# Means of squares: two rounded products with the split squares in place of one float32 product, in a two-layer hybrid trunk

## The chip, the cores and the metric

The kernel runs on 1 core of one Trainium2 chip. The metric is the device time of one execution in microseconds (us). Every row below is from the hardware profile of one execution; PE is TensorE, PEld its weight loads, DVE is VectorE, ACT is ScalarE, POOL is GpSimd, SP is SyncE, which here issues DMAs only.

## The reference, cut to what matters

Two layers over one sequence of 512 tokens of width 1024, all in float32:

```python
for l in range(2):
    x = x + 0.5 * swiglu(rms_norm(x, ffn1_norm[l]), ffn1_w_in[l], ffn1_w_out[l])   # hidden width 2816
    h = rms_norm(x, mix_norm[l]) @ w_mix_in[l]
    y = concat[short_conv(h parts), hgrn2(h parts), forgetting_attention(h parts)]
    x = x + y @ w_mix_out[l]
    x = x + 0.5 * swiglu(rms_norm(x, ffn2_norm[l]), ffn2_w_in[l], ffn2_w_out[l])

def rms_norm(x, gain):
    return x * rsqrt(mean(x * x, axis=-1) + 1e-6) * gain
# hgrn2 ends, for each of 4 heads of width 64:  rms_norm(o, out_gain) * silu(gate)
```

So there are six norms of x (two feed-forwards and a mixer in each of two layers), and a norm of HGRN2's heads in each layer.

## The kernel before

x is held transposed: 8 tiles `xT` of 128 features by 512 tokens, so a mean over features is a sum over partitions, which TensorE does as a product with a matrix of constants (`ones_mean`, 1/1024 everywhere; `ones_blk`, 1/64 in two diagonal blocks, one for each head of a pair).

Large products don't run in float32. Each operand is taken apart into a high part, the value rounded to the type F32R (fp32r in the profile), and a low part, what is missing: a cast on ACT, then a subtraction on DVE (`parted`, lines 398 and 401, for a weight tile `st` into `hl`). A product is then three rounded ones, high x high, low x high, high x low (`mm3`, lines 413, 419, 420). Weights come in pairs of 128 rows: one DMA into the staging buffer `st` (two of these), one cast, one subtraction into `hl` (three of these), and 24 products of 512 columns.

The squares of x are not taken apart. `norm_part` makes, for tile j, the operand's high part `x` = gain * xT on ACT (line 537), its low part on DVE (538), the square on ACT (548 for the first tile, 551 for the others) and on DVE the running sum `sqa` (552). `sum_norm` (line 571) then is one float32 product `ones_mean` x `sqa`, and `take_norm` makes the inverse root of it on ACT and DVE. The scale `inv` is applied to the products behind it, so the products with weights start before the norm is known:

- In a mixer, `features` streams the first four weight pairs, and the sum (`end_norm`) stands ahead of the last pair's products.
- In a feed-forward, `cover` works through the first hidden tiles with pairs of weight rows. Ahead of pair n, `deal(n)` places work by hand: the sum (`squares`) where n is `mean`, which is 2 in the first feed-forward and 3 in the second one; the norm, the other operands and so on from a table by pair.
- In the very first feed-forward of the kernel (`begin` given) the norm has a path of its own.

What sets the order: each engine works through its own queue in program order. `follow` chains instructions of one engine in the order in which the code makes them; in `cover`, the weights' casts and subtractions (`keep` in `parted`), the products and what `deal` places are chained so, while `norm_part`'s squares are placed by the scheduler. Elsewhere the weights' rounding has a high priority, and the scheduler takes it as early as its buffers allow.

The HGRN2 part (`hgrn`) runs as a generator for each pair of heads, beside the attention's projections. It ends with `sq`, the squares of the output, a float32 product `ones_blk` x `sq` (line 1479), the inverse root (`r`, `t`; line 559 is its first DVE step), and the output's two parts `hy`. Behind it in program order comes the attention: the operands `b` from transposes (1597, 1598), DMA copies of them by SP's queue (1605), scores (1632), their negative row maximum `nm` on DVE (1646), the exponential `P` on ACT (309), the values `V` (1570, scaled by `invc` on DVE), transposes (1669) and the products with V (1687).

PSUM holds eight banks under four names, `mm` (3), `sc` (2), `pt` (2) and `po` (1); a product into a bank waits until its former reader is done.

Of the kernel before, what the change touches and what calls it, by code (L numbers as in the profile page):

```python
# [8 lines left out]
F32 = mybir.dt.float32  # L9
F32R = mybir.dt.float32r  # L10
# [15 lines left out]
P = 128  # L26
T = 512
D = 1024
# [155 lines left out]
class Trunk:  # L184
# [8 lines left out]
    def __init__(self, ctx, tc):  # L193
        self.tc = tc
        self.nc = tc.nc
        nc = self.nc
        self.uid = 0
        self.ntog = 0
        self.tab, self.tab_users = None, []
        self.chain = {}  # L200
        self.hl0 = None
        self.const = ctx.enter_context(tc.tile_pool(name="const", bufs=1))
        self.res = ctx.enter_context(tc.tile_pool(name="res", bufs=1))
        self.wp = ctx.enter_context(tc.tile_pool(name="wp", bufs=1))
        self.ps = ctx.enter_context(
            tc.tile_pool(name="ps", bufs=1, space=bass.MemoryType.PSUM)
        )
        self.dram = ctx.enter_context(
            tc.tile_pool(name="dram", bufs=1, space=bass.MemoryType.DRAM)
        )  # L210

        self.none = self.res.tile([P, T], F32R, tag="inv", name="none")
        self.follow("v", nc.vector.memset(self.none.bitcast(F32), 0.0))
        self.ident = self.const.tile([P, P], F32, tag="ident", name="ident")
        make_identity(nc, self.ident)
        self.ones_mean = self.const.tile([P, P], F32, tag="ones_mean", name="ones_mean")
        self.follow("v", nc.vector.memset(self.ones_mean, 1.0 / D))
        self.epsc = self.const.tile([P, 1], F32, tag="epsc", name="epsc")
        nc.vector.memset(self.epsc, EPS)
        self.xT = self.res.tile([P, KD, T], F32, tag="xT", name="xT")  # L220

        self.xh, self.xl = [None] * KD, [None] * KD

    def build_consts(self, scratch):

        nc = self.nc
        c = self.const

        self.ones_blk = c.tile([P, P], F32, tag="ones_blk", name="ones_blk")
        nc.vector.memset(self.ones_blk, 0.0)  # L230
        for h in range(2):
            nc.vector.memset(self.ones_blk[64 * h : 64 * h + 64, 64 * h : 64 * h + 64], 1.0 / 64)

        self.heads2 = c.tile([P, 2], F32, tag="heads2", name="heads2")
        nc.vector.memset(self.heads2, 0.0)
        for h in range(2):
            nc.vector.memset(self.heads2[64 * h : 64 * h + 64, h : h + 1], 1.0)

        self.smask = c.tile([P, T], F32, tag="smask", name="smask")
        nc.vector.memset(self.smask, 1.0)  # L240
        nc.vector.memset(self.smask.rearrange("p (c t) -> p c t", t=CH)[:, :, 0:1], 0.0)
        self.identb = c.tile([P, P], BF16, tag="identb", name="identb")
        nc.vector.tensor_copy(self.identb, self.ident)
        self.utri = c.tile([P, T], F32R, tag="utri", name="utri")
        self.maskb = c.tile([P, P], BF16, tag="maskb", name="maskb")

        self.lmask = c.tile([P, 6, CH], U8, tag="lmask", name="lmask")
        self.same = c.tile([P, CH], F32, tag="same", name="same")
        ft = scratch(I32)[:, :P]
        pt = scratch(I32)[:, :P]  # L250
        nc.gpsimd.iota(ft, pattern=[[1, P]], base=0, channel_multiplier=0)
        nc.gpsimd.iota(pt, pattern=[[0, P]], base=0, channel_multiplier=1)
        ftf = scratch(F32)[:, :P]
        ptf = scratch(F32)[:, :P]
        nc.vector.tensor_copy(ftf, ft)
        nc.vector.tensor_copy(ptf, pt)
        x = scratch(I32)[:, :P]
        nc.vector.tensor_tensor(x, ft, pt, op=ALU.bitwise_xor)
        xf = scratch(F32)[:, :CH]
        later = scratch(F32)[:, : P + CH]  # L260
        later, own = later[:, :P], later[:, P:]
        nc.vector.tensor_tensor(later, ftf, ptf, op=ALU.is_gt)
        for h in range(2):

            r = slice(CH * h, CH * h + CH)
            nc.vector.tensor_copy(xf[r], x[r, r])
            nc.vector.tensor_copy(own[r], later[r, r])
            nc.vector.tensor_copy(self.same[r], self.ident[r, r])
        a = scratch(F32)[:, :CH]
        b = scratch(F32)[:, :CH]  # L270
        for l in range(1, 7):
            i = nc.vector.tensor_scalar(
                a, xf, scalar1=float(2 ** (l - 1)), scalar2=None, op0=ALU.is_ge
            )
            if l == 1:

                self.tc.add_manual_dep(i.ins, self.first_rows, NOSYNC, reason="opening order")
            nc.vector.tensor_scalar(b, xf, scalar1=float(2**l), scalar2=None, op0=ALU.is_lt)
            nc.vector.tensor_mul(a, a, b)
            nc.vector.tensor_mul(self.lmask[:, l - 1, :], a, own)  # L280

        nc.vector.tensor_scalar(self.maskb, later, scalar1=-1e30, scalar2=None, op0=ALU.mult)

        nc.vector.tensor_tensor(self.utri[:, :P], ftf, ptf, op=ALU.is_ge)
        of = scratch(F32)[:, P:]
        nc.vector.memset(of, 1.0)
        nc.vector.tensor_copy(self.utri[:, P:], of)
# [278 lines left out]
    def end_norm(self, bank, pool):  # L566
        self.sum_norm(bank)
        self.take_norm(bank, pool)

    def sum_norm(self, bank):  # L570
        return self.nc.tensor.matmul(bank, self.ones_mean, self.sqacc, start=True, stop=True)

    def take_norm(self, bank, pool):

# [76 lines left out]
    def cover(self, fp, w_in, w_out, covered, mean, begin):  # L651
# [3 lines left out]
        nc = self.nc  # L655
        if begin is not None:
            x, gain = begin
        A, V = (lambda i, e=e: self.follow(e, i) for e in "av")
        norm, tiles, values = [], [], {}
# [20 lines left out]
        def squares():  # L680

            norm.append(self.bank("pt" if self.ntog % 2 == 0 else "po"))
            i = self.sum_norm(norm[0])
            if begin is None:
                self.follow("p", i)

        def deal(n):
            if n == mean and begin is None:
                squares()
            for what in filter(None, ENTRY[covered].get(n, "").split(", ")):  # L690
                name, *at = what.split()
                at = [int(v) if v.isdigit() else v for v in at]
                if name == "norm":
                    for e, i in self.take_norm(norm[0], fp):
                        self.follow(e, i)
                    self.table(SILU)
                    self.signs()
                elif name == "x":
                    self.normalise(fp, *at)
                elif name == "+":  # L700
                    x, y = (self.xn[tuple(v)] for v in (at[:2], at[2:]))
                    V(nc.vector.tensor_add(x, x, y))
                elif name == "clear":
                    clear(*at)
                elif name == "silu":
                    gi = values[at[0]][0]
                    A(self.act(gi, gi, AF.Silu))
                elif name == "values":
                    value(*at)
                elif name == "load":  # L710
                    next(halved)
                elif name == "sum":
                    self.first_sum()
                else:
                    self.operand(fp, name)
# [343 lines left out]
    def mix(self, l, w, w_out, conv_w, out_gain, q_gain, k_gain, f_bias, next_gain, logits):  # L1059
        nc, tc = self.nc, self.tc  # L1060
        FM2 = [slice(0, P), slice(P, 2 * P)]
        TOK = [slice(c, c + P) for c in (0, 128, 256, 384)]
        with tc.tile_pool(name=self.n("mix"), bufs=1) as mp:
# [31 lines left out]
            def features(*args):  # L1095
                g = features_steps(*args)
                while True:
                    try:
                        next(g)
                    except StopIteration as e:  # L1100
                        return e.value
# [10 lines left out]
            with tc.tile_pool(name=self.n("hg"), bufs=1) as hp:  # L1112
                self.tt, self.tb = "t", 8

                b, kb, q, S = (pair(mp, tag) for tag in ("b", "kb", "q", "S"))
                negc = mp.tile([NH, 2, T], F32R, tag="n", name=self.n("negc"))
                bz = features([(H_F, 256)], ("mm", "mm"), lambda: self.end_norm(self.bank("pt"), hp))
                if l == 0:
                    self.lower_bounds(logits, hp.tile([P, T], F32, tag="t", name=self.n("lb"), bufs=8))
# [165 lines left out]
    def hgrn(self, l, pr, hp, z, q, q2, v, sg, og, S, kb, b):  # L1285
# [7 lines left out]
        nc = self.nc  # L1293
# [178 lines left out]
        for par in range(2):  # L1472
            mine = lambda a: a.rearrange("p (i two t) -> p i two t", two=2, t=CH)[:, :, par, :]
            src = ob[par][:, : T // 2].rearrange("p (i t) -> p i t", t=CH)
            nc.scalar.activation(mine(sq), src, AF.Square)
            nc.scalar.copy(mine(o), src)
        yield
        mb = self.bank("sc")
        nc.tensor.matmul(mb, self.ones_blk, sq, start=True, stop=True)
        self.act(r, mb, AF.Ln, bias=self.epsc)  # L1480
        self.act(r, r, AF.Exp, scale=-0.5)
        self.rsqrt(r, mb, r, t)
# [373 lines left out]
```

## Time and profile before

| | |
|---|---|
| median of 3 runs | 1824.36 us (1824.35 to 1825.08) |
| the profiled execution's own time | 1826.36 us |
| its span in the profile | 1824.6 us |
| PE busy | 1816.4 us, 13,237 products |
| PEld busy | 1662.6 us |
| DVE busy | 1436.1 us, 1,971 instructions |
| ACT busy | 1000.3 us, 1,421 instructions |
| POOL busy | 185.2 us |
| granted TensorE clock | 1.00 |
| DMA | 262.43 MB, mean 144 GB/s |

How to read it: the span is the time from the first to the last profiled event on the core. A row of a timeline has the start in us from the span's beginning, the duration, the engine, the line of the kernel, the operation, output<-inputs by the program's names, and shapes; a bracket at its end holds the engine's idle time before the row and what ended it. "x2" behind a matmul says that the instruction stands as two records. Matmuls overlap their predecessors, so what one costs is the distance to its successor's start, not its duration. An `SPq` row is a DMA issue on SP's queue.

### The profile page before, as it was taken

The numbers are of one execution on the slowest core, as the hardware profiler recorded it, in microseconds if no ns is written. First come the engines' busy times: TensorE is split into PE (matmuls) and PEld (weight loads), VectorE is DVE, ScalarE is ACT, GpSimd is POOL, SyncE is SP. The second block draws the span as 40 slices with busy tenths as digits, with TensorE's granted clock in tenths as the row PEclk, the third lists the DMA queues.
The fourth block names the chain that finished last, engine by engine and source line by source line (L and its number), as shares of the span: only waits on it lengthen the run. The fifth ranks groups of instructions, "written<-read, shape, count | busy, mean of one in ns | idle before, by whom it ended". The sixth has DMA issues, their size and how long they took to land.

```text
span 1824.6 us, 32613 instructions
## 1 busy us (share of the span) xinstructions
PE 1816.4 (100%) x13237; PEld 1662.6 (91%) x13237; DVE 1436.1 (79%) x1971; ACT 1000.3 (55%) x1421; POOL 185.2 (10%) x190
## 2 busy tenths in 40 slices
PE   9999999999999999999999999999999999999999
PEld 7899999887888899999889999998878888999998
DVE  7889787678677898879678887976777778888883
ACT  5455554465665465555445555555656655555552
POOL 0011120100000101112001111201000001020210
PEclk9999999999999999999999999999999999999999
DMA  7658784242543867868276787823425438677762
GB/s 213 179 130 193 179 177 98 66 126 78 125 105 96 223 139 163 195 162 170 81 201 140 173 182 195 162 70 77 122 79 127 120 93 219 162 153 195 155 135 93
DMA packets 249911, 262.43 MB, mean 144 GB/s; under 512 B 19816, under 2 KB 228464, under 8 KB 249760
## 3 DMA queue, kind: packets, MB, share of 16 engines
q1 hardware_dynamic: 193904, 192.15, 35.8%
q0 software_dynamic: 55840, 68.19, 23.6%
q8 instruction: 104, 1.70, 0.4%
q14 instruction: 47, 0.39, 0.1%
q10 hardware_dynamic: 16, 0.00, 0.0%
HBM read 226.15 MB, written 2.17 MB: 125 GB/s over the span
## 4 chain that ended last, share of the span: by engine, by line
PE 95%; DVE 1%; ACT 1%; DMA 1%; issue 0%; SPq 0%; ACTq 0%; DVEq 0%
PE mm L413 14%; PE mm L420 14%; PE mm L419 14%; PE sc L413 6%; PE sc L420 6%; PE sc L419 6%; PE pt L419 6%; PE pt L413 6%; PE pt L420 6%; PE po L413 4%; PE po L419 4%; PE po L420 4%; PE sc L1632 1%; PE po L1687 1%; PE pt L1669 1%; DMA st<-in_ffn_w_in_dram 1%
## 5 line engine op out<-in xcount | busy, mean ns | idle before, releaser
L865 ACT CAST hl<-w 128x1024 fp32r<-128x1024 f32 x322 | 337.7, 1050 | 349.5 <-PE mm L420 81.9
L867 DVE TENSOR_TENSOR hl<-w,hl 128x1024 fp32r<-128x1024 f32 x322 | 393.1, 1222 | 87.2 <-ACT hl L865 87.1
L401 DVE TENSOR_TENSOR hl<-st,hl 128x1024 fp32r<-128x1024 f32 (+3 forms) x152 | 160.4, 1055 | 121.7 <-ACT hl L398 121.3
L398 ACT CAST hl<-st 128x1024 fp32r<-128x1024 f32 (+3 forms) x151 | 138.2, 915 | 184.0 <-PE po L420 84.5
L413 PE MATMUL mm<-xc,hl 128*128 128x256 f32 (+1 forms) x730 | 201.3, 276 | 0.3 <-ACT g L964 0.3
L420 PE MATMUL mm<-xc,hl 128*128 128x256 f32 x728 | 201.2, 276 | 0.0
L419 PE MATMUL mm<-xc,hl 128*128 128x256 f32 x728 | 201.1, 276 | 0.0
L413 PE MATMUL sc<-xc,hl 128*128 128x256 f32 (+1 forms) x530 | 146.5, 277 | 0.6 <-ACT g L964 0.6
L420 PE MATMUL sc<-xc,hl 128*128 128x256 f32 x528 | 146.3, 277 | 0.0
L419 PE MATMUL sc<-xc,hl 128*128 128x256 f32 x528 | 146.2, 277 | 0.0
L413 PEld LDWEIGHTS mm<-xc,hl 128*128 128x128 f32 x730 | 137.0, 188 | 0.8 <-ACT g L964 0.5
L420 PEld LDWEIGHTS mm<-xc,hl 128*128 128x128 f32 x728 | 136.6, 188 | 0.1
L419 PEld LDWEIGHTS mm<-xc,hl 128*128 128x128 f32 x728 | 136.7, 188 | 0.0
L419 PE MATMUL pt<-xc,hl 128*128 128x256 f32 x480 | 132.8, 277 | 0.0
L413 PE MATMUL pt<-xc,hl 128*128 128x256 f32 (+1 forms) x482 | 132.8, 276 | 0.0
L420 PE MATMUL pt<-xc,hl 128*128 128x256 f32 x480 | 132.7, 276 | 0.0
L413 PE MATMUL mm<-x,hl 128*128 128x512 f32 x272 | 108.8, 400 | 0.0
L420 PE MATMUL mm<-x,hl 128*128 128x512 f32 x272 | 106.1, 390 | 0.0
L419 PE MATMUL mm<-x,hl 128*128 128x512 f32 x272 | 105.9, 389 | 0.0
L413 PEld LDWEIGHTS sc<-xc,hl 128*128 128x128 f32 x530 | 99.7, 188 | 1.5 <-ACT g L964 1.0
L420 PEld LDWEIGHTS sc<-xc,hl 128*128 128x128 f32 x528 | 99.1, 188 | 0.1
L419 PEld LDWEIGHTS sc<-xc,hl 128*128 128x128 f32 x528 | 99.2, 188 | 0.0
(504 smaller groups left out, 5449.6 us busy)
## 6 DMA issues: line engine op xcount, KB each, us to landing
w<-in_ffn_w_in_dram SPq DMA_DIRECT2D x140, 512.0 KB
w<-in_ffn_w_out_dram SPq DMA_DIRECT2D x64, 512.0 KB
w<-in_ffn_w_out_dram POOLq DMA_DIRECT2D x56, 512.0 KB, 8.8
st<-in_w_mix_in_dram SPq DMA_DIRECT2D x80, 256.0 KB
w<-in_ffn_w_in_dram POOLq DMA_DIRECT2D x39, 512.0 KB, 8.1
st<-in_ffn_w_in_dram SPq DMA_DIRECT2D x70, 256.0 KB
w<-S POOLq DMA_DIRECT2D x35, 512.0 KB, 4.7
st<-in_ffn_w_out_dram SPq DMA_DIRECT2D x24, 512.0 KB
```

Of the source, the lines that this page charges most:

```text
L398: a = nc.scalar.copy(hi, src[:, c : c + w])
L401: b = nc.vector.tensor_sub(lo, src[:, c : c + w], hi)
L413: i = nc.tensor.matmul(acc[:, c], ah, bh[:, c], start=first and c.start == 0, stop=False, skip_group_check=True,)
L419: nc.tensor.matmul(acc, ah, bl, start=False, stop=False, skip_group_check=True)
L420: i = nc.tensor.matmul(acc, al, bh, start=False, stop=last, skip_group_check=True)
L865: A(nc.scalar.copy(hi, src))
L867: return lambda: V(nc.vector.tensor_sub(lo, src, hi))
L1632: mm = lambda *a, **k: E(nc.tensor.matmul(*a, skip_group_check=True, **k))
L1669: E(nc.tensor.transpose(tb[:, k * P : (k + 1) * P], to[u][:, j * P : (j + 1) * P], self.ident))
L1687: E(nc.tensor.matmul(self.ob[:, o], half[2][:, j, h].rearrange("p a d -> p (a d)"), part[:, at[0] : at[-1] + 1, :].rearrange("p b t -> p ( ...
```

## The change

`ones_mean` and `ones_blk` become F32R. The squares' sum `sqa` is taken apart by a cast and a subtraction into two tiles `sp` (`split`), and the sum over partitions becomes two rounded products, `ones` x high and `ones` x low, accumulated in one bank (`sums`). This is done at the norm of both mixers, of both second feed-forwards and of layer 1's first feed-forward (five sums), and at the four sums of HGRN2's heads. The opening norm of the kernel stays a float32 product. In a feed-forward the split is made in `deal(mean - 1)`, and its cast and subtraction are chained into ACT's and DVE's given order there; the products stay at `mean`. In a mixer and in `hgrn` the split isn't chained.

```diff
-        self.ones_mean = self.const.tile([P, P], F32, tag="ones_mean", name="ones_mean")
+        self.ones_mean = self.const.tile([P, P], F32R, tag="ones_mean", name="ones_mean")
...
-        self.ones_blk = c.tile([P, P], F32, tag="ones_blk", name="ones_blk")
+        self.ones_blk = c.tile([P, P], F32R, tag="ones_blk", name="ones_blk")
...
+    def split(self, src, pool):
+        hi, lo = (
+            pool.tile([P, T], F32R, tag=self.tt, name=self.n("sp"), bufs=self.tb) for _ in "hl"
+        )
+        return (hi, lo), self.nc.scalar.copy(hi, src), self.nc.vector.tensor_sub(lo, src, hi)
+
+    def sums(self, bank, ones, parts):
+        return [
+            self.nc.tensor.matmul(
+                bank, ones, x, start=i == 0, stop=i == 1, skip_group_check=True
+            )
+            for i, x in enumerate(parts)
+        ]
+
+    def split_norm(self, pool):
+        self.sqacc, a, v = self.split(self.sqacc, pool)
+        return a, v
+
     def sum_norm(self, bank):
-        return self.nc.tensor.matmul(bank, self.ones_mean, self.sqacc, start=True, stop=True)
+        if isinstance(self.sqacc, tuple):
+            return self.sums(bank, self.ones_mean, self.sqacc)
+        return [self.nc.tensor.matmul(
+            bank, self.ones_mean.bitcast(F32), self.sqacc, start=True, stop=True
+        )]
...
         def squares():
             norm.append(self.bank("pt" if self.ntog % 2 == 0 else "po"))
-            i = self.sum_norm(norm[0])
-            if begin is None:
-                self.follow("p", i)
+            for i in self.sum_norm(norm[0]):
+                if begin is None:
+                    self.follow("p", i)
 
         def deal(n):
+            if n == mean - 1 and begin is None:
+                for e, i in zip("av", self.split_norm(fp)):
+                    self.follow(e, i)
             if n == mean and begin is None:
                 squares()
...
+                self.split_norm(hp)
                 bz = features([(H_F, 256)], ("mm", "mm"), lambda: self.end_norm(self.bank("pt"), hp))
...
             nc.scalar.copy(mine(o), src)
+        parts = self.split(sq, hp)[0]
         yield
         mb = self.bank("sc")
-        nc.tensor.matmul(mb, self.ones_blk, sq, start=True, stop=True)
+        self.sums(mb, self.ones_blk, parts)
```

The chaining moves instructions far from the ones that are added. ACT's row at the start of layer 0's second feed-forward, before: `hl_6456` is the weight pair 1, `hl_6486` pair 2, `hl_6518` pair 3 and `hl_6552` the one behind; the `x` and `sq` rows are `norm_part`'s.

```order
L398 CAST hl_6486<-st_6483 128x1024
L537 ACTIVATE x_911_6346<-xT,gain_5053 128x512
L551 ACTIVATE sq_6349<-xT 128x512
L537 ACTIVATE x_919_6387<-xT,gain_5053 128x512
L551 ACTIVATE sq_6390<-xT 128x512
L398 CAST hl_6518<-st_6515 128x1024
L537 ACTIVATE x_921_6394<-xT,gain_5053 128x512
L551 ACTIVATE sq_6397<-xT 128x512
L537 ACTIVATE x_923_6401<-xT,gain_5053 128x512
L551 ACTIVATE sq_6404<-xT 128x512
L537 ACTIVATE x_925_6408<-xT,gain_5053 128x512
L551 ACTIVATE sq_6411<-xT 128x512
```

After, the end of the same stretch (lines are numbered anew: 398 is 399, 537 is 538, 551 is 552; `hl_6505`, `hl_6538` and `hl_6572` are the pairs 2, 3 and the one behind, `sp` is the split's high part):

```order
L538 ACTIVATE x_927_6409<-xT,gain_5068 128x512
L552 ACTIVATE sq_6412<-xT 128x512
L538 ACTIVATE x_929_6416<-xT,gain_5068 128x512
L552 ACTIVATE sq_6419<-xT 128x512
L538 ACTIVATE x_931_6423<-xT,gain_5068 128x512
L552 ACTIVATE sq_6426<-xT 128x512
L576 CAST sp_6498<-sqa_6344 128x512
L399 CAST hl_6505<-st_6502 128x1024
L399 CAST hl_6538<-st_6535 128x1024
L399 CAST hl_6572<-st_6569 128x1024
```

The casts of the pairs 2 and 3, which stood among the squares, stand behind the last square and the split now; the subtractions on DVE follow them.

DVE's row in layer 0 from the last step of the second head pair (`hy`) to the first attention head's maxima, before (`hl_5392` is a weight pair of the mixer's input projection):

```order
L1488 TENSOR_TENSOR hy_5018<-t_4987,hy_5018 128x512
L1598 SCALAR_TENSOR_TENSOR b_659_5118<-pt_5125,qkg_3691,b_658_5117 128x512
L1646 TENSOR_REDUCE nm_5102<-sc_5104 128x1
L1570 SCALAR_TENSOR_TENSOR V_4770<-mm_4773,invc_3905,V_4770 128x8x64
L401 TENSOR_TENSOR hl_5392<-st_5389,hl_5392 128x1024
L1646 TENSOR_REDUCE nm_5102<-sc_5104 128x1
L1570 SCALAR_TENSOR_TENSOR V_4770<-po_4774,invc_3905,V_4770 128x8x64
```

And after:

```order
L1629 SCALAR_TENSOR_TENSOR b_665_5133<-pt_5140,qkg_3691,b_664_5132 128x512
L1515 SCALAR_TENSOR_TENSOR t_4996<-t_4996,og_3690,sg_3901 128x512
L1601 SCALAR_TENSOR_TENSOR V_4775<-mm_4777,invc_3910,V_4775 128x8x64
L1601 SCALAR_TENSOR_TENSOR V_4775<-mm_4778,invc_3910,V_4775 128x8x64
L1519 TENSOR_TENSOR hy_5033<-t_4996,hy_5033 128x512
L402 TENSOR_TENSOR hl_5407<-st_5404,hl_5407 128x1024
L1677 TENSOR_REDUCE nm_5117<-sc_5119 128x1
L1601 SCALAR_TENSOR_TENSOR V_4775<-po_4779,invc_3910,V_4775 128x8x64
L1677 TENSOR_REDUCE nm_5117<-sc_5119 128x1
```

Two rows of the values V moved ahead of the maxima: one ahead of `hy` and one between the two `nm`, which stood behind them before.

More of the change, by code (lines that the diff above doesn't have):

```diff
@@ L215, in __init__ @@
         make_identity(nc, self.ident)
-        self.ones_mean = self.const.tile([P, P], F32, tag="ones_mean", name="ones_mean")
-        self.follow("v", nc.vector.memset(self.ones_mean, 1.0 / D))
+        self.ones_mean = self.const.tile([P, P], F32R, tag="ones_mean", name="ones_mean")
+        self.follow("v", nc.vector.memset(self.ones_mean.bitcast(F32), 1.0 / D))
         self.epsc = self.const.tile([P, 1], F32, tag="epsc", name="epsc")
@@ L227, in build_consts @@
         c = self.const
-        self.ones_blk = c.tile([P, P], F32, tag="ones_blk", name="ones_blk")
-        nc.vector.memset(self.ones_blk, 0.0)
+        self.ones_blk = c.tile([P, P], F32R, tag="ones_blk", name="ones_blk")
+        blk = self.ones_blk.bitcast(F32)
+        nc.vector.memset(blk, 0.0)
         for h in range(2):
-            nc.vector.memset(self.ones_blk[64 * h : 64 * h + 64, 64 * h : 64 * h + 64], 1.0 / 64)
+            nc.vector.memset(blk[64 * h : 64 * h + 64, 64 * h : 64 * h + 64], 1.0 / 64)
         self.heads2 = c.tile([P, 2], F32, tag="heads2", name="heads2")
```

## The prediction

> **What bounds the kernel now.** I read the profile's page first: the busy times of the engines and the chain that ended last.
>
> ```profile
> PE 1816.4 (100%) x13237; PEld 1662.6 (91%) x13237; DVE 1436.1 (79%) x1971; ACT 1000.3 (55%) x1421; POOL 185.2 (10%) x190
> ...
> PE 95%; DVE 1%; ACT 1%; DMA 1%; issue 0%; SPq 0%; ACTq 0%; DVEq 0%
> ```
>
> TensorE (PE) is busy for the whole span and is 95% of the chain. So a microsecond taken from PE's queue is a microsecond won, and a microsecond for which PE must wait is lost, since no idle time stands anywhere to absorb it. Hence two questions: how much PE time do the nine changed sums give back, and does any operand now reach PE late? The next view is the timeline of PE at a sum of each kind: for the heads (`ones_blk`, line 1479) and for a norm (`ones_mean`, line 571).
>
> ```profile
> 461.19 1.08 PE L1479 MATMUL sc<-t,ones_blk 128*128 128x512 f32 x2
> 462.10 0.27 PE L1594 MATMUL pt<-ident,qk 128*128 128x128 f32 x1
> ...
> 600.24 0.39 PE L413 MATMUL sc<-x,hl 128*128 128x512 f32 x1
> ...
> 605.69 1.02 PE L571 MATMUL po<-sqa,ones_mean 128*128 128x512 f32 x2
> 606.15 0.79 PE L413 MATMUL sc<-x,hl 128*128 128x512 f32 x1
> 606.78 0.40 PE L419 MATMUL sc<-x,hl 128*128 128x512 f32 x1
> 607.01 0.39 PE L420 MATMUL sc<-x,hl 128*128 128x512 f32 x1
> ```
>
> From one start to the next, a rounded product of 512 columns holds PE for 0.23 us (606.78 to 607.01). The float32 sum of a norm holds it from 605.69 to 606.55 (606.78 less the 0.23 of the product before it): 0.86 us. The heads' sum takes 0.91 (461.19 to 462.10).
>
> **What the change removes.** In place of each sum stand two rounded products, 0.46. Saved: 0.40 at each of five norms, 0.45 at each of four head sums: 2.0 + 1.8 = 3.8 us, if nothing waits. That is the most that can be won. [...]
>
> **What it adds.** Nine casts on ScalarE (ACT) and nine subtractions on VectorE (DVE), 128x512 each. At the norm inside each mixer the rows of the same size stand side by side (ACT, DVE and PE views, layer 0):
>
> ```profile
> 346.44 0.62 ACT L398 CAST hl<-st 128x512 fp32r<-128x512 f32 x1 [1.34 <-PE mm L420]
> ```
>
> ```profile
> 345.75 0.68 DVE L552 TENSOR_TENSOR sqa<-sqa,sq 128x512 f32<-128x512 f32 x1
> 347.10 0.69 DVE L401 TENSOR_TENSOR hl<-st,hl 128x512 fp32r<-128x512 f32 x1 [0.67 <-ACT hl L398]
> ```
>
> ```profile
> 348.97 0.59 PE L571 MATMUL pt<-sqa,ones_mean 128*128 128x512 f32 x1
> ```
>
> So a split costs 0.62 + 0.69. Here it is hidden: the squares are whole at 346.43; the cast follows the weight cast of 346.44 in ACT's queue (about 347.0 to 347.6), the subtraction follows (to 348.4), and PE wants the sum at 348.97. Its cover is the 2.7 us in which PE works through one more pair of rows (12 products of 0.23); without it PE would wait 1.3. Two mixers: -0.8 us.
>
> **The split in the feed-forward layers** is chained into the hand-made order of ACT and DVE one weight pair ahead of the sum. In the second feed-forward of a layer the cast of pair 2 now stands behind the split, and so behind the very last square. What it did before (ACT's timeline, then DVE's):
>
> ```profile
> 589.56 1.06 ACT L398 CAST hl<-st 128x1024 fp32r<-128x1024 f32 x1 [0.93 <-PE po L420]
> ```
>
> ```profile
> 590.78 1.22 DVE L401 TENSOR_TENSOR hl<-st,hl 128x1024 fp32r<-128x1024 f32 x1
> 591.92 0.75 DVE L538 SCALAR_TENSOR_TENSOR x<-xT,gain,x 128x512 fp32r<-128x512 f32 x1
> ...
> 600.57 0.69 DVE L552 TENSOR_TENSOR sqa<-sqa,sq 128x512 f32<-128x512 f32 x1
> ```
>
> Pair 2 was rounded at 589.56 to 592.00, and PE first reads it at 600.24 (the quoted row): over 8 us early. Now DVE does its norm work first. Between 590.78 and the last square's end at 601.26 it loses two weight subtractions, 1.14 each from start to start (590.78 to 591.92), so that the last square would end at 598.98; going through the rows one after another, ACT's steps between give back 0.27: 599.25. Then ACT: split cast from 599.28, weight cast 0.53 behind it (casts of 512 overlap their successor by 0.09), 599.81 to 600.87; DVE subtracts for the low part from 600.90 to 602.13. PE's third product of the pair needs that low part at 600.24 + 2 x 0.23 = 600.70. PE waits about 1.45, and something more for loading the weights it waited for: an estimate of 1.6, between 1.2 and 2.0. The sum behind it then waits for nothing. Each of two such layers: 1.6 - 0.4 = +1.2; together +2.4.
>
> In the first feed-forward of layer 1 the sum is one pair earlier, so pair 1 stands behind the split:
>
> ```profile
> 911.13 1.05 ACT L398 CAST hl<-st 128x1024 fp32r<-128x1024 f32 x1 [4.38 <-PE pt L420]
> ```
>
> ```profile
> 912.22 1.23 DVE L401 TENSOR_TENSOR hl<-st,hl 128x1024 fp32r<-128x1024 f32 x1 [4.21 <-ACT hl L398]
> 913.37 1.28 DVE L644 SCALAR_TENSOR_TENSOR xT<-sc,xT 128x512 f32<-128x512 f32 x2
> ...
> 922.52 0.69 DVE L552 TENSOR_TENSOR sqa<-sqa,sq 128x512 f32<-128x512 f32 x1
> ```
>
> ```profile
> 921.82 0.39 PE L413 MATMUL mm<-x,hl 128*128 128x512 f32 x1
> ```
>
> The last square ended at 923.21. Two subtractions out of the way are 2 x 1.15 (912.22 to 913.37), 0.15 comes back as waits: 921.06. Split cast 921.09, weight cast 921.62 to 922.68, low part to 923.94; PE wants the high part at 921.82 and the low one at 922.28. It waits 0.9, then to about 924: 1.7, with the weight load 1.9 (1.3 to 2.4). Less 0.4: +1.5.
>
> Queued behind the late casts are the casts of pairs 3 and 4 and, on SyncE's queue, the loads that wait for their staging buffers; 5.4 us of products per pair (24 x 0.23) cover these, and the norm that now runs a few microseconds later has four pairs, 21 us, before PE needs its result. I cost them at nothing; if that cover fails, the next weights are late by about the load's length, and that is in the rival below.
>
> [...] No row here shows an ACT row overtaking another.
>
> **The heads.** Two sums in a row give PE 2 x 0.45 = 0.9 back, and the low parts arrive as PE reaches them, because transposes and four products are now ordered between. The new wait lies 16 us on, at the first attention head's second scores:
>
> ```profile
> 466.82 0.68 DVE L559 SCALAR_TENSOR_TENSOR t<-sc,t 128x512 f32<-128x512 f32 x1
> ...
> 476.76 1.22 DVE L401 TENSOR_TENSOR hl<-st,hl 128x1024 fp32r<-128x1024 f32 x1 [0.49 <-ACT hl L398]
> 477.90 0.42 DVE L1646 TENSOR_REDUCE nm<-sc 128x1 f32<-128x256 f32 x1
> 478.23 0.74 DVE L1570 SCALAR_TENSOR_TENSOR V<-po,invc,V 128x512 fp32r<-128x512 f32 x1
> ```
>
> ```profile
> 478.97 0.51 PE L1632 MATMUL sc<-A 128*128 128x512 f32 x1 [0.19 <-ACT P L309]
> ...
> 492.26 0.30 PE L1632 MATMUL sc<-A 128*128 128x128 f32 x1
> 492.63 0.30 PE L1632 MATMUL sc<-kb,kb 66*128 66x128 f32 x1
> ```
>
> PE at 478.97 already waits (for the bank that the exponential reads, which waits for the maximum `nm` of 477.90): 0.4. After the change DVE starts the second head sum's row (466.82) 0.5 later, since ACT has one more cast ahead of it; from there to `nm` it is DVE that is full, now with the values' row of 478.23 (0.66 to its successor's start) ahead of `nm` and the old idle 0.5 and 0.1 gone. So `nm` comes at about 478.4 and PE starts at 479.4: 0.5 later than before instead of 0.9 earlier. Part comes back at 492.26 and 492.63, where PE waited 0.3 and 0.3 for copies that SyncE issued last at
>
> ```profile
> 488.67 0.59 SPq L1605 DMA_DIRECT2D kb<-b  x1
> ```
>
> These copies stand ahead of a weight load now and are issued some 0.4 earlier, while PE comes 0.5 later. I take the pair of sums at -0.1 to +0.1 in each layer, 0 in all; bounds are -0.9 (no wait) and +0.6 (nothing comes back).
>
> **The sum.** Mixers -0.8, second feed-forwards +2.4, first feed-forward +1.5, heads 0: +3.1 us. The profiled execution took 1826.36 with a span of 1824.6; the median of the runs is 1824.36, and all within 0.04%. The difference holds for either, so I forecast 1824.4 + 3.1 = **1827.5 us**, 0.17% more. Taking the lower and upper bounds together the forecast's own case runs from -0.8 + 2 x 0.8 + 0.9 - 1.8 = -0.1 to -0.8 + 2 x 1.6 + 2.0 + 1.2 = +5.6. A measurement of this kernel tells about 0.2% (3.65 us) from no change, so even a forecast that is right may come out as slower.
>
> **Rivals.** First, slower: the cover of the loads fails. A late low part also frees the staging buffer late (in layer 0 at 602.1 in place of 592.0), two 512 KB loads of the next stage now stand ahead of the load it releases, and if this pair is late at PE by one weight cast and subtraction (1.06 + 1.22 = 2.3 us) in each of the three feed-forwards, 6.9 come on top: about 1834.5; with one of three 1829.8. It decides where the load lands over 5 us after its turn. Against it: PE needs that pair 11 us after its buffer comes free. 15%.
>
> Second, faster: DVE and ACT clear the norm before PE gets there, and the full 3.8 us are won: 1820.6. For it speaks that over 8 us of slack stand there now; against it, that all of this slack lies ahead of the last square, and the last square is bound by DVE's own rows. 5%.
>
> Third, the compiler's two products take 0.43 each as the two halves of the float32 ones do, because the operand's type is not what sets the pass: the saving is zero and the waits stay, 1827.5 + 3.8 = 1831.3. Against it: the products with `hl` are of the new type, and hold PE for 0.23. 3%.
>
> The forecast has the remaining 77%. **Numbers:** of its range about a third lies above +3.65 and nearly nothing below -3.65. Slower by over 0.2%: 0.77 x 0.38 + 0.15 + 0.03 = 0.47; faster 0.05; within 0.2%: 0.48. The range that holds 8 of 10 reaches from 1824.0, just under the forecast's lower bound of 1824.4 - 0.1, to 1831.0, into the slower rivals.
>
> **What would show it.** Right: sums of 0.46 on PE; PE idle of 1.2 to 2.4 us at the third weight pair of each layer's second feed-forward and at the second pair of layer 1's first, ended by DVE's `hl`; a wait of over 1 us at the second scores of the first head; no wait at the mixers' sums. Wrong: PE without a gap at those pairs (then the faster rival), or gaps also at the following pairs, ended by a DMA (the slower one).

## The result and the profile after

The changed kernel takes 1829.23 us (median of 10 runs, 1827.16 to 1831.72) against 1824.45 us of the kernel before (10 runs beside it): the ratio is 1.0023, with a 95% interval of 1.0015 to 1.0031, that is 2.7 to 5.7 us more. It is slower, by little more than the 0.2% that a measurement of this kernel can tell. The profiled execution has a span of 1827.4 us.

The page's busy times and chain of the changed kernel:

```profile
PE 1812.6 (99%) x13237; PEld 1660.5 (91%) x13237; DVE 1442.7 (79%) x1980; ACT 1005.6 (55%) x1430; POOL 184.8 (10%) x190
...
PE 90%; DVE 5%; ACT 3%; DMA 1%; issue 1%; SPq 0%; ACTq 0%; DVEq 0%
```

PE is busy for 3.8 us less than before, and the span is 2.8 us longer: PE waits now, and DVE and ACT have 8 points of the chain in place of 2. Where it waits shows in the table of stretches. Its columns are the stretch, its length, busy time and instructions of PE, PEld, DVE, ACT and POOL, granted clock, DMA share and GB/s; first the kernel before, then the changed one, in the stretches around the sums of the first two feed-forwards concerned:

```profile
598.00:610.00 12.00, 12.00 (x53) 9.59 (x52) 5.54 (x9) 5.65 (x9) 1.30 (x1) 1.00 0.69 205
920.00:930.00 10.00, 10.00 (x44) 7.94 (x43) 4.87 (x6) 4.66 (x7) 1.30 (x1) 1.00 0.61 187
```

```profile
598.00:610.00 12.00, 10.83 (x47) 8.28 (x46) 5.37 (x7) 5.74 (x8) 1.30 (x1) 1.00 0.82 233
920.00:930.00 10.00, 8.66 (x37) 6.49 (x36) 4.94 (x6) 3.75 (x5) 1.30 (x1) 1.00 0.72 214
```

PE had no idle time there before and has 1.2 and 1.3 us now. The timelines of the changed kernel in layer 0's second feed-forward name the wait (ACT, then DVE, then PE):

```profile
597.30 0.61 ACT L552 ACTIVATE sq<-xT 128x512 f32<-128x512 f32 x1
599.06 0.62 ACT L576 CAST sp<-sqa 128x512 fp32r<-128x512 f32 x1 [1.15 <-issue]
599.59 1.99 ACT L399 CAST hl<-st 128x1024 fp32r<-128x1024 f32 x2
```

```profile
598.23 0.68 DVE L553 TENSOR_TENSOR sqa<-sqa,sq 128x512 f32<-128x512 f32 x1
599.72 0.69 DVE L576 TENSOR_TENSOR sp<-sqa,sp 128x512 fp32r<-128x512 f32 x1 [0.81 <-ACT sp L576]
600.66 2.36 DVE L402 TENSOR_TENSOR hl<-st,hl 128x1024 fp32r<-128x1024 f32 x2 [0.25 <-ACT hl L399]
```

```profile
600.68 0.50 PE L414 MATMUL sc<-x,hl 128*128 128x512 f32 x1 [0.64 <-ACT hl L399]
601.02 0.39 PE L420 MATMUL sc<-x,hl 128*128 128x512 f32 x1
601.94 0.51 PE L421 MATMUL sc<-x,hl 128*128 128x512 f32 x1 [0.53 <-DVE hl L402]
602.28 0.40 PE L414 MATMUL sc<-x,hl 128*128 128x512 f32 x1
...
607.11 0.63 PE L581 MATMUL po<-sp,ones_mean 128*128 128x512 f32 x2
607.58 0.40 PE L414 MATMUL sc<-x,hl 128*128 128x512 f32 x1
```

ACT stands idle for 1.15 us behind the last square (597.30), until DVE's last addition is done at 598.91 (the profile names no releaser here; at the same row of layer 1, at 921.28, it names DVE's `sqa`); then come the split's cast and only then the weight cast of pair 2. PE waits twice, for the high part and for the low part. The two rounded sums take 0.47 us (607.11 to 607.58). The same pair of waits stands at 922.89 and 924.15 and at 1504.29 and 1505.54.

**Place by place.** The products stand in nearly the same order in all traces, so the start of a product in one trace less its start in the trace of the kernel before gives the time lost up to there; its growth over a place is what that place costs (the same place agrees to about 0.03 us between kernels where no DMA is near; at the attention's start kernels move by up to 0.4 without a change there). For the changed kernel:

| place | predicted | by the traces |
|---|---|---|
| mixer of layer 0: sum | -0.4 | -0.39 |
| the same mixer, 26 us later | 0 | +0.37 |
| mixer of layer 1: sum | -0.4 | -0.21 |
| layer 0, second feed-forward: wait, sum | +1.6, -0.4 | +1.78, -0.39 |
| layer 1, first feed-forward: wait, sum | +1.9, -0.4 | +1.94, -0.39 |
| layer 1, second feed-forward: wait, sum | +1.6, -0.4 | +1.74, -0.39 |
| heads of layer 0, of layer 1 | 0, 0 | -0.20, +0.06 |
| sum | +3.1 | +3.9 |

The spans differ by 2.8 and not by 3.9, because of slower stretches that come and go without regard to the edit (last section): the profiled execution of before holds one more of them, about 1 us.

### The profile page after: what moved, and what is told of

Read it like the earlier page. It is cut to its first block, busy times and chain, and to the rows that moved or that the text cites. A ratio compares the mean times of both kernels' runs of the same rounds, so it can differ in the third digit from the quotient of the medians.

```text
span 1827.4 us, 32637 instructions
## 1 busy us (share of the span) xinstructions
PE 1812.6 (99%) x13237; PEld 1660.5 (91%) x13237; DVE 1442.7 (79%) x1980; ACT 1005.6 (55%) x1430; POOL 184.8 (10%) x190
## 4 chain that ended last, share of the span: by engine, by line
PE 90%; DVE 5%; ACT 3%; DMA 1%; issue 1%; SPq 0%; ACTq 0%; DVEq 0%
PE mm L414 14%; PE mm L421 13%; PE mm L420 13%; PE sc L421 6%; PE sc L414 6%; PE sc L420 6%; PE pt L420 5%; PE pt L414 5%; PE pt L421 5%; PE po L414 3%; PE po L420 3%; PE po L421 3%; PE sc L1663 1%; DVE hl L402 1%; PE po L1718 1%
```

## Experiments

Each kernel was timed in five rounds beside the kernel before. Ratios are to that one; intervals are of 95%.

**Heads alone, norms alone.** The change is undone in the norms (the split and its order) or in the heads (`sums` back to a float32 product):

```diff
-            if n == mean - 1 and begin is None:
-                for e, i in zip("av", self.split_norm(fp)):
-                    self.follow(e, i)
...
-                self.split_norm(hp)
```

```diff
-        parts = self.split(sq, hp)[0]
...
-        self.sums(mb, self.ones_blk, parts)
+        nc.tensor.matmul(mb, self.ones_blk.bitcast(F32), sq, start=True, stop=True)
```

> Only the four sums of the heads are two rounded products; the norms keep the float32 product. Theory A (the loss is the order of the weight pairs in the feed-forwards): nothing to lose there, and in the heads 4 x 0.45 = 1.8 us saved and about as much waited for at the second scores of the first attention head: -0.5 to +0.2 us against the kernel before. Theory B (the loss comes from the added casts and subtractions, wherever they stand, or from the products themselves): four of the nine splits, so about four ninths of +4.8 us: +2.1 us.

> Only the five norms are changed, the heads keep the float32 product. Theory A: all the loss is here: mixers -0.8, three feed-forwards +4.3 to +5.5, together +3.5 to +4.7 us against the kernel before. Theory B: five ninths of +4.8: +2.7 us.

Measured: heads 1.0004 (0.9995 to 1.0013), norms 1.0025 (1.0015 to 1.0036), that is +4.6 us. By the table of places: heads -0.20 and +0.04; norms +1.75, +1.93, +1.73 at the three pairs, as in the full change. The loss is in the norms. For the heads both theories' numbers lie in the interval (-0.9 to +2.4 us); the places decide for the first.

**The split one pair later.** The split is made just ahead of its products, so the weights of pair `mean - 1` are rounded among the squares again:

```diff
-            if n == mean - 1 and begin is None:
+            if n == mean and begin is None:
                 for e, i in zip("av", self.split_norm(fp)):
                     self.follow(e, i)
-            if n == mean and begin is None:
                 squares()
```

> The change as it is, but in the feed-forwards the split is made in deal(mean), just ahead of its products, and so behind the rounding of pair mean - 1 and ahead of that of pair mean. Theory A: pair mean - 1 is rounded among the squares as before, PE has over 2 us between the last square and the sum, and the next pair is rounded before PE is through with the sum: the waits of 1.5 to 2.0 us at three pairs vanish, and each sum gives 0.4 back: 1824.4 - 5 x 0.4 - about 0.2 in the heads = 1822.2 us, 2 us less than the kernel before and 6 to 7 us less than the change as it is. Theory B: nothing taken away: still +4 to +5 us.

Measured: 0.9993 (0.9984 to 1.0002). All three waits are gone (0.00 in the table of places), and each of the five sums gives 0.39 back:

```profile
606.23 0.40 PE L421 MATMUL pt<-x,hl 128*128 128x512 f32 x1
606.47 0.62 PE L581 MATMUL po<-sp,ones_mean 128*128 128x512 f32 x2
606.93 0.40 PE L414 MATMUL sc<-x,hl 128*128 128x512 f32 x1
```

With the same splits and the same work, only in another order, the loss has gone. That falls against the theory that the added work costs. Its sum over the places is -1.7 us; the time alone does not tell it from no change.

**The order alone.** The kernel before, with nothing added but two orderings: the first weight cast of pair `mean - 1` behind the last square on ACT, its subtraction behind the last addition on DVE (`last` holds these two; the lines in which `norm_part` notes them and `follow` obeys are left out here).

```diff
+            if n == mean - 1 and begin is None:
+                self.behind = dict(self.last)
```

> The kernel before with one thing added: in the three feed-forwards concerned the rounding of pair mean - 1 is ordered behind the last square (ACT) and the last addition of the squares' sum (DVE). No split, all sums in float32. Theory A: by the trace of the changed kernel the last sum of squares ends at 598.91 in layer 0's second feed-forward, so the low part comes at about 601.3 where PE needs it at 600.70: 0.7 us lost, twice; in layer 1's first one at about 923.6 where it is needed at 922.28: 1.3 us: together +2.5 to +3 us, about two thirds of what the splits and the order cost together. Theory B: no work is added, so 0 us.

Measured: 1.0001 (0.9992 to 1.001), and 0.0 lost at both pairs of the second feed-forwards, 0.2 at the first one. My expectation was wrong. I had let the weight cast wait for the last addition, but this order only sets it behind the last square:

```profile
596.54 0.62 ACT L556 ACTIVATE sq<-xT 128x512 f32<-128x512 f32 x1
597.06 1.98 ACT L403 CAST hl<-st 128x1024 fp32r<-128x1024 f32 x2
```

The cast begins at 597.06, while DVE still adds (to 598.15 in this trace), and DVE's subtraction follows the addition without a gap: just in time. So the place among the squares is not what costs. What remains is that ACT, working in order, waits for DVE ahead of the weight cast.

**That wait alone.** The kernel before, no split, all sums in float32; ACT only reads one column of the squares' sum ahead of the weight cast. First with a small tile of its own for that column, then with a column of a buffer that is there anyway (the second diff shows what differs from the first):

```diff
+            if n == mean - 1 and begin is None:
+                one = fp.tile([P, 1], F32, tag="one", name=self.n("one"))
+                A(nc.scalar.copy(one, self.sqacc[:, :1]))
```

```diff
-                one = fp.tile([P, 1], F32, tag="one", name=self.n("one"))
-                A(nc.scalar.copy(one, self.sqacc[:, :1]))
+                one = fp.tile([P, T], F32, tag="g2", name=self.n("one"), bufs=2)
+                A(nc.scalar.copy(one[:, :1], self.sqacc[:, :1]))
```

> The kernel before (all sums in float32, no split), with one narrow read added on ACT in each of the three feed-forwards: a copy of one column of the squares' sum, chained ahead of the rounding of pair mean - 1, so that the weight cast waits for DVE's last addition. Theory A2 (the loss comes from the weight cast standing behind a wait for the last addition in ACT's queue, the split's own cast adding 0.5 us to it): PE loses 1.1 us at the pair in each second feed-forward and 1.5 in layer 1's first one, together +3 to +4.5 us, with no work added to speak of. Theory B (the added work of the splits): 0.

> As wait_only (the kernel before, with one column of the squares' sum read on ACT ahead of the rounding of pair mean - 1), but the copy goes into a column of a buffer that the pool has anyway, so no tile changes its place. Theory A2: only the waits at the three pairs are left, 1.0 to 1.3 us each: +3 to +4 us. Theory E (the wait itself, not the added tile, slowed the products of the stage behind it): again +30 us or more.

Measured: 1.0194 (1.018 to 1.0208) with the tile, 1.0027 (1.0016 to 1.0037), +4.9 us, without. The second is the clean one: the added wait with no added tile. It has the two waits of the changed kernel at the same products:

```profile
599.71 0.19 ACT L690 COPY one<-sqa 128x1 f32<-128x1 f32 x1 [1.15 <-issue]
599.81 1.99 ACT L398 CAST hl<-st 128x1024 fp32r<-128x1024 f32 x2
```

```profile
600.90 0.50 PE L413 MATMUL sc<-x,hl 128*128 128x512 f32 x1 [0.21 <-ACT hl L398]
601.24 0.40 PE L419 MATMUL sc<-x,hl 128*128 128x512 f32 x1
602.16 0.50 PE L420 MATMUL sc<-x,hl 128*128 128x512 f32 x1 [0.52 <-DVE hl L401]
```

The three places cost 1.33, 1.50 and 1.35 us, a little more than the 1.0 to 1.3 expected: three quarters of the 1.78, 1.94 and 1.74 of the change, from 0.2 us of added work each. The split's own cast ahead of the weights (599.06 to 599.59, 0.53, less the column's 0.1) is the last quarter. What the tile did in the first version is told in the last section.

**The split on POOL.** The change with cast and subtraction of the feed-forwards' splits on POOL, and the weights in the order of the "order alone" kernel:

```diff
-                for e, i in zip("av", self.split_norm(fp)):
-                    self.follow(e, i)
+                hi, lo = (fp.tile([P, T], F32R, tag=self.tt, name=self.n("sp"), bufs=self.tb) for _ in "hl")
+                nc.gpsimd.tensor_copy(hi, self.sqacc)
+                nc.gpsimd.tensor_sub(lo, self.sqacc, hi)
+                self.sqacc = hi, lo
+                self.behind = dict(self.last)
```

> The change, but in the feed-forwards the split's cast and subtraction run on POOL, and the rounding of pair mean - 1 keeps its place behind the last square and the last addition, as in order_only. Theory A2: the weight cast no longer waits behind the split, so PE loses nothing at that pair, and the sums, two POOL steps behind the last addition, are still in time: as late_split, 1822 to 1823 us with the clean clock (about 2 us less than before). Theory B2 (the place behind the last square is enough, with DVE as the bound): waits of 1 us or more stay at the three pairs, +2 us or more.

Measured: 1.0000 (0.9991 to 1.0009). The waits at the pairs are gone (0.00, 0.23, 0.06), although the cast takes 1.44 us and the subtraction 2.15 on POOL. With the one-column kernel this shows that what made PE wait is ACT's queue, in which the weight cast stood behind a step that waited for DVE. The 2 us that I expected beside it did not come: two later places lose 0.5 us each more than with the late split, and why is open.

**The heads.** Before PE reaches the second scores of the first attention head, DVE works without a gap. In the changed kernel (DVE, then ACT, then PE):

```profile
476.17 1.22 DVE L402 TENSOR_TENSOR hl<-st,hl 128x1024 fp32r<-128x1024 f32 x1
477.31 0.28 DVE L1677 TENSOR_REDUCE nm<-sc 128x1 f32<-128x128 f32 x1
477.51 0.74 DVE L1601 SCALAR_TENSOR_TENSOR V<-po,invc,V 128x512 fp32r<-128x512 f32 x1
478.17 0.88 DVE L1677 TENSOR_REDUCE nm<-sc 128x1 f32<-128x256 f32 x2
```

```profile
478.62 0.47 ACT L310 ACTIVATE P<-sc,nm 128x256 f32<-128x256 f32 x1 [0.53 <-DVE nm L1677]
```

```profile
477.65 0.23 PE L1663 MATMUL sc<-maskb,identb 128*128 128x128 bf16 x1
479.24 0.50 PE L1663 MATMUL sc<-A 128*128 128x512 f32 x1 [1.36 <-ACT P L310]
```

PE waits for the exponential `P`, and that waits for DVE's maximum `nm`.

Three kernels ask whether DVE's full queue is the cause: two move the heads' last subtraction to POOL (one on top of the late split, one in the kernel before), and one, on top of the late split, leaves a DVE step out, the product with gain and gate.

```diff
-        nc.vector.tensor_sub(self.yl[2 + pr], o, self.yh[2 + pr])
+        nc.gpsimd.tensor_sub(self.yl[2 + pr], o, self.yh[2 + pr])
```

```diff
-        nc.vector.scalar_tensor_tensor(out=o, in0=o, scalar=og, in1=sg, op0=ALU.mult, op1=ALU.mult)
```

> late_split, with the low parts of the heads' outputs (hy, two subtractions of 0.68 us on DVE per layer) on POOL. Theory C (after the heads' sums it is DVE's queue, full from the second sum's row to the first maximum of the attention, that makes PE wait 1.4 us at the second scores): 0.7 to 1.4 us come off DVE ahead of the maxima, and the wait shrinks to 0.5 or less: 0.8 to 1.2 us less than late_split in each layer, 1.6 to 2.4 in all. Rival D (the wait stands for something else, ACT's exponential or the scores' transfers): the same wait, the time of late_split.

> The kernel before with the low parts of the heads' outputs on POOL. Theory C: PE's wait at the second scores is only 0.4 us there, so at most 0.4 us in each layer can be won: -0.8 to 0 us. So of what late_pool wins, more than half is won only behind the rounded sums. Rival D: 0.

> late_split, with one step of the heads' outputs left out: the product with gain and gate, one DVE row of 0.75 us for each pair of heads, two in each layer. Theory C (DVE's full queue between the second sum's row and the attention's first maxima makes PE wait at the second scores): 1.4 us of 10 gone there, and the order lets the maxima pass a weight subtraction, so the wait of 1.4 us at the second scores shrinks to under 0.4: 1 us less than late_split in each layer. Rival D (it waits for something else): the wait stays.

Measured: 1.0003 (0.9994 to 1.0012), 1.0001 (0.9992 to 1.001) and 0.9975 (0.9966 to 0.9984). The step moved to POOL did not relieve DVE, so these kernels do not test the theory: behind the late split the wait at the scores was 1.58 us. A DVE row that takes 0.68 in the kernel before (469.02) took 1.79 beside POOL's subtraction, and the maximum came behind 0.80 of idle time that the profile puts down to POOL's `hy`:

```profile
469.53 1.79 DVE L564 TENSOR_TENSOR t<-t,t 128x512 f32<-128x512 f32 x1
...
476.02 0.29 DVE L1676 TENSOR_REDUCE nm<-sc 128x1 f32<-128x128 f32 x1 [0.80 <-POOL hy L1518]
```

```profile
469.34 1.44 POOL L1518 TENSOR_TENSOR hy<-t,hy 128x512 fp32r<-128x512 f32 x1 [31.06 <-ACT hy L1517]
```

With the step left out the wait is gone, and the heads win 1.88 and 1.59 us where the late split won 0.20 and lost 0.06: 1.7 more in each layer, about the wait with its restart (477.65 to 479.24 above, 1.6). Not the two DVE rows of 0.75 us alone decide over it: in this trace the maxima also stand ahead of a weight subtraction of 1.23 us, behind which the late split has them. Both shorten what stands ahead of the maxima in DVE's queue, and that is the cause.

**Two last kernels.** The late split without the heads' part, and the late split with the heads' output multiplied by gain and gate ahead of the norm's factor, where DVE is idle, in place of behind it:

```diff
         parts = self.split(sq, hp)[0]
+        nc.vector.scalar_tensor_tensor(out=o, in0=o, scalar=og, in1=sg, op0=ALU.mult, op1=ALU.mult)
...
-        nc.vector.scalar_tensor_tensor(out=o, in0=o, scalar=og, in1=sg, op0=ALU.mult, op1=ALU.mult)
```

> late_split without the heads' part: their four sums stay float32 products. By the steps so far the heads' rounded sums win 0.9 us in each layer and lose it at the second scores, so this kernel takes what late_split takes, within 0.6 us, and 1 to 2 us less than the kernel before. If the heads' part is a real gain (or loss), it is 1 us or more away from late_split.

> late_split, with the product of the heads' output with gain and gate moved ahead of the norm's factor (o*gain*gate first, the inverse root after it): nothing left out, but two DVE rows of 0.75 us per layer stand now where DVE idles before the sums, not between the second sum's row and the first maxima. Theory C: the wait at the second scores vanishes as it did with that step left out (heads -1.9 and -1.6 us by the trace there), so about 3.5 us less than late_split's -1.7: -4 to -5.5 us against the kernel before, 1819.5 to 1821 us. Rival D2 (there the step's absence itself won, not its place): the time of late_split, -1.7.

Measured: 0.9994 (0.9985 to 1.0003) and 0.9981 (0.9972 to 0.999). The first agrees with the late split: the heads' rounded sums alone win nothing. The second is faster than the changed kernel and than the kernel before, by 3.5 us (1.8 to 5.1) against the latter; its places add up to -4.1 (heads -1.59 and -1.46). It loses 0.89 at the later place of layer 0's mixer, as two other kernels did, and not 0.37; why is open. Its second scores follow the first without a wait:

```profile
478.21 0.23 PE L1662 MATMUL sc<-maskb,identb 128*128 128x128 bf16 x1
478.25 0.48 PE L1662 MATMUL sc<-A 128*128 128x512 f32 x1
```

It has the same number of rows as the late split. Two of them per layer stand at another place, and so does the weight subtraction, which follows the maximum here:

```profile
475.71 0.42 DVE L1676 TENSOR_REDUCE nm<-sc 128x1 f32<-128x256 f32 x1
476.60 1.23 DVE L402 TENSOR_TENSOR hl<-st,hl 128x1024 fp32r<-128x1024 f32 x1 [0.47 <-ACT hl L399]
```

Whether the same move wins as much with the float32 sums of the kernel before was not run.

## Why the prediction was right

I forecast 1827.5 us with a range to 1831.0; 1829.23 lies in it, on the slow side. The sum of the terms was +3.1, the places give +3.9: the mixers won 0.2 in place of 0.8, the three waits cost 0.4 more, and the heads won 0.1.

- **The saving.** 0.39 us for each norm against 0.40: right. For the float32 product the chain of the kernel before has 0.86 at all five sums (349.13, 605.85, 927.43, 1250.83 and 1506.61), the price that I had taken from one row.
- **The feed-forwards.** The mechanism is the one predicted, row by row: the last addition, forecast to end at 599.25, ended at 598.91 (598.23 + 0.68); the split's cast followed at 599.06, the weight cast at 599.59, and PE waited for the high and the low part. The terms were mis-sized by little: 1.78 and 1.74 for 1.6, 1.94 for 1.9. Of the 1.78, 1.61 are lost when the third product starts, the one that needs the low part; I had forecast 1.45. What I left too small is the handing over between engines: from the last addition's end to that product I had counted 2.88 us (599.25 to 602.13), and it was 3.03 (598.91 to 601.94), above all because ACT began 0.15 behind the addition and not 0.03. The restart is the rest, 0.17 for 0.15, which was my estimate: the product behind this wait held PE for 0.34 us, not 0.23 (601.94 to 602.28). That counts once, since PE waits for the low part whatever the first restart takes. The waits rest on ACT's rows running in the order given, and the one-column kernel shows that at work: its weight cast starts at 599.81, just behind the copy of 599.71 that had waited 1.15, while with no wait ahead of it (the order alone) it starts at 597.06.
- **The mixers.** This term failed: -0.23 in place of -0.8. In layer 0 the 0.39 was taken back 26 us later. DVE's row there before, then in the changed kernel with the row of PE that waits for it:

```profile
374.65 0.68 DVE L1144 TENSOR_TENSOR q<-mm,inv 128x512 f32<-128x512 f32 x1
```

```profile
374.56 0.69 DVE L1174 TENSOR_TENSOR q<-mm,inv 128x512 f32<-128x512 f32 x1
...
375.30 0.19 PEld L414 LDWEIGHTS mm<-hl,x 128*128 128x128 f32 x1 [0.38 <-DVE q L1174]
```

 Before, PE came to this bank at 375.42, when DVE was just done (375.33). DVE's row moved by 0.09 us and PE by 0.45, so a PE that comes earlier only waits. I had looked for covers around the split, not for the next place where PE is just in time. In layer 1 half of the 0.4 went at the sum itself. I had priced both mixers by the rows of layer 0, where the weight cast ahead of the split starts 2.53 us before the sum (346.44 to 348.97). In layer 1 it waits for its load, before and after:

```profile
1249.42 0.62 ACT L398 CAST hl<-st 128x512 fp32r<-128x512 f32 x1 [2.62 <-DMA st<-in_w_mix_in_dram]
```

```profile
1251.60 0.62 ACT L399 CAST hl<-st 128x512 fp32r<-128x512 f32 x1 [2.17 <-DMA st<-in_w_mix_in_dram]
...
1252.86 0.68 DVE L576 TENSOR_TENSOR sp<-sqa,sp 128x512 fp32r<-128x512 f32 x1
...
1253.60 0.19 PEld L581 LDWEIGHTS pt<-sp,ones_mean 128*128 128x128 f32 x1 [0.35 <-DVE sp L576]
```

 Before, PE's sum of layer 1 started at 1250.67, 1.25 us behind the cast. In the changed kernel the low part was done at 1253.54, just too late for the second product, and the two took 0.64 us in place of 0.47. It seems to hang on when the load lands: in the other seven kernels with this split the same sum gives 0.39 to 0.41, and in the late split its cast starts 2.40 us ahead of the sum.
- **The heads.** Right in sum (0 forecast, -0.20 and +0.06) and in place: PE starts the second scores at 479.24, forecast 479.4. The experiments confirm the reason, DVE's full queue. That the sum agrees to 0.2 is in part luck, since kernels without a change there move by up to 0.4.
- **The rivals.** The loads' cover held: no further waits at the following pairs. That the type does not set a product's time is out: the two rounded products took 0.47, the float32 one 0.86. The rival with the full saving of 3.8 us would have needed the split behind the weight casts; even that kernel wins 1.7, since one mixer's 0.4 and the heads' 1.8 are waited for elsewhere.

The interval of the measurement (2.7 to 5.7) holds both the forecast's 3.1 and the places' 3.9; it does not tell them apart.

## What to carry to other kernels

An instruction that waits costs what is queued behind it (1.33 to 1.50 us at each of three places, for a copy of 0.19): before a cheap step is chained into an engine's order, ask for the time at which its input is ready, and put it behind everything that is ready earlier and needed sooner. Where the bounding engine has no idle time, time saved on it is won only if the next engine that it meets just in time also moves (0.37 of 0.39 us was taken back 26 us later); look for those places downstream. A step of a busy engine that can be done earlier, where that engine idles, may be worth more than the products saved: here the heads won 1.59 and 1.46 us with it, and 0.20 and -0.06 without.

## What the runs showed beyond that

**One small tile slowed the products behind it.** With the 128x1 tile added, the same stretch holds 4% fewer products (before, then with the tile):

```profile
650.00:850.00 200.00, 200.00 (x1764) 199.83 (x1763) 171.45 (x180) 109.72 (x125) 33.56 (x28) 1.00 0.78 172
```

```profile
650.00:850.00 200.00, 200.00 (x1692) 200.00 (x1691) 164.32 (x172) 105.81 (x121) 32.29 (x27) 1.00 0.73 164
```

A product of 256 columns took 118 ns in place of 113 here (200 us by 1,692 and by 1,764), at a granted clock of 1.00. The span was about 30 us longer than with the same wait and without the tile (1857.5 against 1827.6), beside the 4 us of the three waits that both have; 4% of three stages of some 250 us (630 to 882 in the kernel before) would make that, an estimate from this one stretch. How the tile does it is not shown.

**The same 4% comes and goes in four stretches.** At the end of each feed-forward's long stage some 28 us can run at that rate, about 1 us lost. In the kernel before, then in the changed one:

```profile
857.00:883.00 26.00, 26.00 (x223) 26.00 (x222) 21.90 (x25) 16.56 (x18) 0.00 (x0) 1.00 0.17 40
1188.00:1210.00 22.00, 22.00 (x195) 21.96 (x195) 18.55 (x22) 12.74 (x14) 0.00 (x0) 1.00 0.15 30
```

```profile
857.00:883.00 26.00, 26.00 (x230) 25.94 (x229) 22.43 (x26) 16.58 (x18) 0.00 (x0) 1.00 0.20 43
1188.00:1210.00 22.00, 22.00 (x189) 22.00 (x189) 17.98 (x20) 13.60 (x16) 0.00 (x0) 1.00 0.13 25
```

Which of the four are slow differs between kernels without regard to the edit (one to three in a trace). It makes the spans of two single profiles incomparable to 1 us or more, which is why the places were compared. Its cause stays open.

**A DVE row beside a POOL row.** A DVE row of 0.68 us took 1.79 (469.53 to 471.32) beside a subtraction of 1.44 on POOL (469.34 to 470.78; the heads' section). From its start to POOL's end is 1.25 us, and with its own 0.68 that would be 1.93: the row took nearly as long as if it had waited for POOL's end. What held it back is not shown; it rests on one row, and no run varied it.

**PE after a longer wait.** In the kernel with the step on POOL, PE waited 1.58 us at the second scores of layer 0, and the products behind it held PE for 0.42 us each in place of 0.23, seven of them between these two:

```profile
479.59 0.63 PE L420 MATMUL mm<-x,hl 128*128 128x512 f32 x1
...
482.56 0.39 PE L421 MATMUL mm<-x,hl 128*128 128x512 f32 x1
```

The granted clock was halved for that time (the columns are those of the table of stretches):

```profile
479.00:482.50 3.50, 3.50 (x10) 2.80 (x10) 1.25 (x5) 2.68 (x6) 0.66 (x1) 0.51 0.41 140
482.50:490.00 7.50, 7.50 (x47) 6.17 (x46) 4.66 (x11) 4.38 (x10) 0.45 (x1) 1.00 0.38 102
```

In layer 1 the same wait of 1.58 us had no such result. What lowered the clock in layer 0 for these 3.5 us is not shown.
